# A layer kernel's stretch from the output projection to the third pair, written out in order, with the shift added in place on ScalarE and two weight blocks split ahead

## The chip, the cores and the metric

The kernel runs on one core of a Trainium2 chip. The metric is the device time of one execution in microseconds (us); the median of three runs stands for a kernel. A profile is taken of one execution; its durations are of that execution. A core has five engines that run their own instruction streams and wait for each other through semaphores: TensorE (PE, the matmuls), VectorE (DVE), ScalarE (ACT), GpSimd (POOL) and SyncE (SP, which here issues transfers). Matmuls accumulate in PSUM banks, all other tiles lie in SBUF.

## The reference, cut to what matters

One transformer layer on 512 latent tokens of width 2048. After the two attention branches come the output projection, a modulated norm and a gated MLP:

```
mod_x = (silu(c) @ w_ada + b_ada)                 # 6 x 2048 values
sh1, s1, g1, sh2, s2, g2 = split(mod_x, 6)
...
x = x + g1 * (merged_heads @ w_o)                 # output projection
h2 = rmsnorm(x, norm2_w) * (1 + s2) + sh2
g, u = split(h2 @ w_up, 2)                        # 2 x 5632 columns
g = conv3(g, conv_w) + conv_b                     # over tokens
x = x + g2 * ((silu(g) * u) @ w_down)
out = rmsnorm(x, final_w)
```

## The kernel before

**Numbers in two parts.** Activations are kept transposed: a tile is 128 features by 512 tokens. Every 32-bit matmul operand is split into a high part (a cast, on ScalarE) and a low part (the difference, on VectorE), and a product is three matmuls: high by high, weight high by activation low, weight low by activation high (`mm3`, L104 to L109). A weight block is 128 by 1024: `wblock` loads it (tile `wr`) and splits it (`wh`, `wl`; `split`, L80 and L81).

**Output projection (L1100 to L1125).** Four groups `g` of 512 output features, each over 8 weight blocks `kb`; a block is 24 matmuls of 512 columns. Between the blocks VectorE reduces rows of w_ada (`next_gemv`, L174), 28 of them in this loop, 7 in the last group. At a group's end VectorE adds the gated result to the residual (L1120, tiles `x1`), ScalarE squares it (L1083) and GpSimd sums the squares into `ss`; the last group's four squares are left for the norm.

**Norm (`token_norm`, L1086 to L1098).** A matmul with a matrix of ones sums `ss` and the last four squares over the features (L1090, L1094; 32-bit, two passes each), and `rstd` makes the inverse root: two ScalarE and four VectorE instructions (L162 to L167). The result is `nr`.

**First pair (`first_pair`, L1189 to L1205).** The MLP works on pairs `ft` of a 128-wide gate and a 128-wide value column block. The first two pairs are computed together, over 8 weight blocks taken as 0, 4, 1, 5, 2, 6, 3, 7; a block is 96 matmuls of 256 columns, since the left and right token halves (`h0`, `h1`) have operands of their own. Ahead of each half block `normed` (L1152) makes one feature tile `h` (L1156, VectorE), its high halves with the shift added (L1160, ScalarE) and its low halves (L1161, VectorE). `sums` (L1165) makes four combinations of the two token halves of tiles j and j+8 for later (`t1` to `t4`, each split), needed by the other pairs.

**Third pair and the rest.** Pair 2 is computed in the same way from four more blocks ("u" jobs). From pair 3 on a pair takes 7 products of half the size, Strassen-Winograd style ("p" jobs with k = 0 to 6), whose weight operands are blocks or sums of blocks (`weight_sum`, L1313). Products k = 0, 2 and 6 all add into one PSUM tile `y`; after k = 0 and k = 2 ScalarE copies `y` aside (`kept`, L1301, tile `m`), and the next product into `y` can only start after that copy. A gate goes through `gate_in` (L1214, ScalarE), `convolve` (L1219, L1221, VectorE), `silu` (L1226, ScalarE), `multiply` (L1230 VectorE, L1232 ScalarE) and `finish` (L1236, VectorE).

**What sets the order.** Up to the end of `first_pair` a scheduler places instructions on the engines, from the order of the code, pools and dependences. From L1293 on the order of PE, ACT, DVE and SP is that of the code: job i runs while `cast` (L1347) and `low` (L1353) split the weights of job i+2. Each engine takes its instructions strictly in order.

Of the kernel before, what the change touches and what calls it, by code (L numbers as in the profile page):

```python
# [17 lines left out]
P = 128  # L18
D = 2048
# [33 lines left out]
def layer_kernel(ctx: ExitStack, tc: tile.TileContext, small, rope, c_row, cc_row, x_t, ctx_t, ada, ada_k,  # L53
# [1009 lines left out]
    aq_ = tc.alloc_tile_pool(name="aq2", bufs=16, side="right", reuse_waits="tile")  # L1063

    def q2k(dt=F32):
        return aq_.tile([P, 512], dt, tag="q2k", name=nm("q2k"))

    wo = tc.alloc_tile_pool(name="wo", bufs=1, reuse_waits="tile")
# [4 lines left out]
    for h in range(16):  # L1073
        hl = a2k(F32R), q2k(F32R)
        split(hl[0], hl[1], oraw[h])
        osp.append(hl)

    def add_square(pool, ss, x, first):
        if first:
            sc.square(ss, x)  # L1080
        else:
            q = pool.tile([P, T], F32, tag="sq", name=nm("sq"), bufs=2)[:, :x.shape[1]]
            sc.square(q, x)  # L1083
            gp.tensor_tensor(out=ss, in0=ss, in1=q, op=ALU.add)

    def token_norm(pool, ss, last):  # L1086

        n = ss.shape[1]
        po = b_tile()[:, :n]
        pe.matmul(po, ones32, ss, start=True, stop=False)  # L1090
        for i, x in enumerate(last):
            q = pool.tile([P, T], F32, tag="h", name=nm("sq"), bufs=5)[:, :n]
            sc.square(q, x)
            pe.matmul(po, ones32, q, start=False, stop=i == len(last) - 1)  # L1094
        r = pool.tile([P, T], F32, tag="nr", name=nm("nr"), bufs=1)[:, :n]
        t1, t2 = (pool.tile([P, T], F32, tag="h", name=nm("n"), bufs=5)[:, :n] for _ in range(2))
        rstd(r, po, D, t1, t2)
        return r  # L1098

    x1, ss = [], wo.tile([P, T], F32, name="ss")  # L1100
    for g in range(4):
        if g % 2:
            outs = [b_tile() for _ in range(4)]
        else:
            s0, s1 = s_tile(), s_tile()
            outs = [s0[:, :512], s0[:, 512:], s1[:, :512], s1[:, 512:]]
        for kb in range(8):
            if kb > 2 and g == 0 or g in (1, 2) or kb < 7 and g == 3:
                next_gemv(wo, 1)
            wh, wl = wblock(w_o[g, kb])  # L1110
            order = [(j, i) for j in range(2) for i in range(4)]
            for j, i in sorted(order, key=lambda t: t[1]) if kb == 7 else order:
                kt, o = kb * 2 + j, j * 512 + i * P
                mm3(outs[i], (wh[:, o:o + P], wl[:, o:o + P]), osp[kt], kt == 0, kt == 15)
        for i in range(4):
            dt = g * 4 + i
            xr = wo.tile([P, T], F32, tag="xr", name=nm("xr"), bufs=6)
            nc.sync.dma_start(xr, x_t[dt])
            x = b2k()
            ve.scalar_tensor_tensor(out=x, in0=outs[i], scalar=modx[:, 32 + dt:33 + dt], in1=xr,  # L1120
                                    op0=ALU.mult, op1=ALU.add)
            x1.append(x)
            gp.dma_start(x1_d[dt], x)
            if g < 3:
                add_square(wo, ss, x, dt == 0)  # L1125
# [3 lines left out]
    db = sm.tile([P, 8], F32, name="db")  # L1129
    ve.tensor_tensor(db, modx[:, 56:64], modx[:, 48:56], op=ALU.add)  # L1130
    wo.release()
    ps_b.release()
    ps_s.release()
    nb[0] = 3
    ps_b = ctx.enter_context(tc.tile_pool(name="ps_m", bufs=4, space=PSUM, reuse_waits="tile"))

    ff = tc.alloc_tile_pool(name="ff", bufs=1, reuse_waits="tile")
    hp = tc.alloc_tile_pool(name="hp", bufs=1, side="right", reuse_waits="tile")
    h0, h1 = slice(0, HT), slice(HT, T)
    r = token_norm(hp, ss, x1[12:])
# [3 lines left out]


    hf, hx, t1, t2, t3, t4 = ([None] * KT for _ in range(6))  # L1150

    def normed(kt):  # L1152

        b = modx[:, 48 + kt:49 + kt]
        h = hf[kt] = hp.tile([P, T], F32, tag="h", name=nm("h"), bufs=5)
        ve.scalar_tensor_tensor(out=h, in0=x1[kt], scalar=a2[:, kt:kt + 1], in1=r, op0=ALU.mult, op1=ALU.mult)  # L1156
        hx[kt] = (a2k(F32R), q2k(F32R) if kt >= 8 else hp.tile([P, T], F32R, tag="h12", name=nm("h12"), bufs=8))
        for t, c in zip(hx[kt], (h0, h1)):
            hh, hl = half(t)
            sc.activation(hh, h[:, c], AF.Identity, bias=b)  # L1160
            ve.scalar_tensor_tensor(out=hl, in0=h[:, c], scalar=b, in1=hh.bitcast(F32), op0=ALU.add, op1=ALU.subtract)  # L1161

    spare = [tp.tile([P, T], F32R, tag="tp", name=nm("tp")) for _ in range(8)]

    def sums(j):  # L1165

        a, c, b = hf[j], hf[j + 8], modx[:, 56 + j:57 + j]
        d1, d2 = (hp.tile([P, HT], F32, tag="d", name=nm("d"), bufs=2) for _ in range(2))

        def put_away(t, src):  # L1170
            t[j] = q2k(F32R) if t is t1 else spare.pop(0) if spare else b2k(F32R)
            split(*half(t[j]), src)
# [507 lines left out]
```

## Time and profile before

| | |
|---|---|
| median of 3 runs | 2396.55 us (2394.12 to 2396.8) |
| the profiled execution: its own time | 2392.88 us |
| its span | 2391.1 us |
| granted TensorE clock, mean | 0.996 |
| last group's two last blocks, norm, first and third pair | about 990 to 1085 us of the span |

The page's first part gives the busy time of each engine over the span. PE is the engine with the largest share, and PEld (its weight loads) runs beside it. A timeline row gives start, duration, engine, line, operation, output and inputs, and in brackets the time for which the engine was idle just before and what it was released by. A window row gives length, then busy time with the number of instructions for PE, PEld, DVE, ACT and POOL, then the granted TensorE clock (1.00 is full), the share of the DMA engines that were busy, and GB/s.

### The profile page before, as it was taken

The page shows a single profiled execution, that of the slowest core. Times are in us where ns is not written, and L with a number is a line of the kernel's source. Part 1 is how long each engine was busy: PE and PEld are TensorE (multiplying, and loading weights), DVE is VectorE, ACT ScalarE, POOL GpSimd, SP SyncE. Part 2 cuts the span into 40 slices and gives each one's busy share as a digit, 9 for nine tenths or more (in the row PEclk, how much of TensorE's full clock was granted, in tenths as well). Part 3 has the DMA queues.
Part 4 walks back from the last instruction along what each step waited for, and adds up shares of the span by engine and source line. Part 5 has one row for each costly group of instructions (what it writes and reads, how often), then busy time and mean ns, then how long its engine had stood idle before and what let it go on. Part 6 is the DMA issues. An engine that isn't in the chain of part 4 may idle for free.

```text
span 2391.1 us, 32351 instructions
## 1 busy us (share of the span) xinstructions
PE 2331.0 (97%) x12444; PEld 1961.2 (82%) x12444; DVE 1778.5 (74%) x2303; ACT 1100.7 (46%) x1660; POOL 270.2 (11%) x322
## 2 busy tenths in 40 slices
PE   8999999999899999999999999999999999999997
PEld 5787888777677788798888888888888888888887
DVE  5996886798877877697585858575757676767767
ACT  4322322455555622364454545454545454445453
POOL 0011000121100011200101010101010101011113
PEclk9999999999999999999999999999999999999999
DMA  9767777853301289623646464546555545465572
GB/s 382 284 217 279 297 295 282 234 151 110 132 30 49 71 309 359 211 79 125 156 127 150 123 150 128 143 128 142 139 141 138 145 123 151 123 159 123 144 212 76
DMA packets 141515, 407.45 MB, mean 170 GB/s; under 512 B 14881, under 2 KB 31793, under 8 KB 130737
## 3 DMA queue, kind: packets, MB, share of 16 engines
q1 hardware_dynamic: 107584, 300.51, 37.9%
q0 software_dynamic: 32624, 103.83, 18.1%
q8 instruction: 97, 1.59, 0.3%
q10 hardware_dynamic: 1152, 1.05, 0.1%
q14 instruction: 58, 0.47, 0.1%
HBM read 335.86 MB, written 69.48 MB: 170 GB/s over the span
## 4 chain that ended last, share of the span: by engine, by line
PE 85%; DVE 8%; ACT 3%; issue 3%; DMA 1%; POOL 1%; DVEq 0%; SPq 0%; ACTq 0%; POOLq 0%
PE y L1377 13%; PE b L107 10%; PE b L108 10%; PE b L109 10%; PE z L1377 6%; PE y L1379 6%; PE z L1379 3%; PE s L883 3%; PE s L108 3%; PE s L107 3%; PE s L109 3%; PE x L1377 2%; PE x L1379 1%; PE pt L895 1%; PE f L107 1%
## 5 line engine op out<-in xcount | busy, mean ns | idle before, releaser
L1398 POOL DMA_DIRECT2D x_d<-xs x160 | 140.7, 1017 | 1160.4 <-ACT xs L1397 1140.8
L107 PE MATMUL b<-ah,wh 128*128 128x512 f32 (+1 forms) x672 | 259.1, 386 | 0.0
L108 PE MATMUL b<-al,wh 128*128 128x512 f32 (+1 forms) x672 | 259.0, 385 | 0.0
L109 PE MATMUL b<-ah,wl 128*128 128x512 f32 (+1 forms) x672 | 258.0, 384 | 0.0
L1353 DVE TENSOR_TENSOR wl<-rb,wh 128x1024 fp32r<-128x1024 f32 x124 | 151.2, 1220 | 128.7 <-ACT wh L1347 128.7
L1353 DVE TENSOR_TENSOR wl<-wr,wh 128x1024 fp32r<-128x1024 f32 x126 | 153.8, 1221 | 123.0 <-ACT wh L1347 123.0
L1347 ACT CAST wh<-wr 128x1024 fp32r<-128x1024 f32 x126 | 132.3, 1050 | 200.9 <-PE b L108 100.5
L1347 ACT CAST wh<-rb 128x1024 fp32r<-128x1024 f32 x124 | 130.2, 1051 | 191.7 <-PE b L108 116.1
L1353 DVE TENSOR_TENSOR wl<-ws,wh 128x1024 fp32r<-128x1024 f32 x123 | 150.1, 1221 | 89.2 <-ACT wh L1347 89.2
L174 DVE CUSTOM_DVE_ANT_0 ada<-ada,cb,smt 128x2048 f32<-128x2048 f32 x64 | 154.3, 2413 | 50.9 <-DMA ada<-in_ada 50.6
L1347 ACT CAST wh<-ws 128x1024 fp32r<-128x1024 f32 x123 | 128.3, 1043 | 135.7 <-PE b L108 45.4
L109 PEld LDWEIGHTS b<-ah,wl 128*128 128x128 f32 x672 | 126.3, 188 | 25.5
L107 PEld LDWEIGHTS b<-ah,wh 128*128 128x128 f32 x672 | 126.6, 188 | 22.9
L108 PEld LDWEIGHTS b<-al,wh 128*128 128x128 f32 x672 | 126.6, 188 | 22.0
L107 PE MATMUL b<-a2k,wh 128*128 128x512 f32 (+1 forms) x352 | 134.5, 385 | 7.3 <-ACT a2k L1160 5.0
L109 PE MATMUL b<-a2k,wl 128*128 128x512 f32 (+1 forms) x352 | 132.7, 377 | 0.7 <-DVE wl L402 0.6
L80 ACT CAST wh<-wr 128x1024 fp32r<-128x1024 f32 (+2 forms) x64 | 64.3, 1004 | 147.2 <-DMA wr<-in_w_o 45.7
L1377 PE MATMUL y<-b2k,wh 128*128 128x512 f32 x410 | 106.8, 390 | 0.0
L885 DVE TENSOR_REDUCE m<-s 128x1 f32<-128x768 f32 x96 | 90.2, 949 | 20.0 <-PE s L883 19.7
L81 DVE TENSOR_TENSOR wl<-wr,wh 128x1024 fp32r<-128x1024 f32 (+2 forms) x64 | 79.9, 1249 | 29.7 <-ACT wh L80 29.2
L1397 ACT ACTIVATE xs<-b,modx 128x512 f32<-128x512 f32 x160 | 101.0, 680 | 0.1
L210 ACT CAST wh<-wr 128x1024 fp32r<-128x1024 f32 x38 | 40.0, 1052 | 127.8 <-PE b L109 46.3
(536 smaller groups left out, 6080.5 us busy)
## 6 DMA issues: line engine op xcount, KB each, us to landing
rb<-in_w_up SPq DMA_DIRECT2D x123, 512.0 KB, 4.4
ada<-in_ada POOLq DMA_DIRECT2D x52, 1024.0 KB, 6.1
wr<-in_w_dn SPq DMA_DIRECT2D x84, 512.0 KB, 4.0
x_d<-xs POOLq DMA_DIRECT2D x160, 256.0 KB, 6.1
ada<-in_ada SPq DMA_DIRECT2D x28, 1024.0 KB, 6.9
wr<-in_w_up SPq DMA_DIRECT2D x53, 512.0 KB, 4.2
wr<-in_w_f SPq DMA_DIRECT2D x34, 512.0 KB, 5.9
adak<-in_ada_k SPq DMA_DIRECT2D x64, 256.0 KB, 5.4
```

The lines of the kernel that those rows point to most:

```text
L81: ve.tensor_tensor(dst_l, src, dst_h.bitcast(F32), op=ALU.subtract)
L107: pe.matmul(out, st[0], mv[0], start=start, stop=False, **kw)
L108: pe.matmul(out, st[0], mv[1], start=False, stop=False, **kw)
L109: pe.matmul(out, st[1], mv[0], start=False, stop=stop, **kw)
L174: ve.tensor_tensor_reduce(out=junk, in0=w, in1=vec, op0=ALU.mult, op1=ALU.add, scale=1.0, scalar=col("b_ada", j), accum_out=dst[:, j:j + 1])
L885: ve.tensor_reduce(out=m, in_=s[:, :TT], axis=AX.X, op=ALU.max, negate=True)
L1347: sc.copy(hi, raw)
L1353: ve.tensor_tensor(lo, raw, hi.bitcast(F32), op=ALU.subtract)
L1377: pe.matmul(o, w[j][0], hs[j], start=start and j == 0, stop=False, skip_group_check=True)
L1379: pe.matmul(o[:, h0], w[j][1], hs[j][:, h0], start=False, stop=j == 7, skip_group_check=True)
L1397: sc.mul(x, po, modx[:, 80 + dt:81 + dt])
L1398: gp.dma_start(x1_d[dt], x, accum_op=ALU.add)
```

## The change

- The order from the last group of the output projection to the third pair's last "u" block is now written out by hand (`every` engine), joined to the hand order that was there.
- In the last group, blocks 6 and 7 are run for the left token half first, then for the right. Residual, squares, ones matmuls, root and the first two normed pairs of tiles are done by halves too.
- `normed` now makes a pair of tiles: the norm, the left high half with bias, then the shift is added to the whole tile in place by ScalarE (`with_shift`, L1168), the right high half is a plain cast (L1184), and the low halves are plain differences (L1190). `sums` takes the shifted tiles, so its four combinations are plain additions and differences of 256 columns (L1204 to L1207); their splits are four casts and four differences in two separate pieces (`first`, `second`) that the order places with `some`.
- The third pair's first two weight blocks are loaded and split during the first pair. The loads of w_ada rows in the last group are issued ahead.
- The gates of the first three pairs, the weight sums and casts of pair 3 are placed by hand up to product k = 0 of pair 3 (`run(4)`); after it the loop is as before. The tile pools are cut differently to hold this.

The diff, cut to its core:

```diff
+
+    h0, h1 = slice(0, HT), slice(HT, T)
+    UP = [kb for j in range(4) for kb in (j, j + 4)]
...
+
+    def load8(i):
+        if i < len(src8):
+            raw8[i] = wraw(src8[i])
...
+        hl8[i] = [(pool or wp).tile([P, 1024], F32R, tag=g, name=nm(g), bufs=2 if pool else 3) for g in ("wh", "wl")]
+        sc.copy(hl8[i][0], raw8[i])
+
+    def low8(i):
+        ve.tensor_tensor(hl8[i][1], raw8.pop(i), hl8[i][0].bitcast(F32), op=ALU.subtract)
+        load8(i + 3)
+
...
-                mm3(outs[i], (wh[:, o:o + P], wl[:, o:o + P]), osp[kt], kt == 0, kt == 15)
+            out_block(outs, kb, wblock(w_o[g, kb]), skip=False)
+        if g == 2:
+            for i in range(2):
+                hl8[i] = wblock(src8[i])
         for i in range(4):
...
-            ve.scalar_tensor_tensor(out=hl, in0=h[:, c], scalar=b, in1=hh.bitcast(F32), op0=ALU.add, op1=ALU.subtract)
-
-    spare = [tp.tile([P, T], F32R, tag="tp", name=nm("tp")) for _ in range(8)]
+    hx, ht, t1, t2, t3, t4 = ([None] * KT for _ in range(6))
+
...
+    def norm_in(kt, c=slice(0, T)):
+        if ht[kt] is None:
+            ht[kt] = tp2k() if kt >= 8 else q2k(0)
+            hx[kt] = a2k(F32R), q2k(1, F32R) if kt >= 8 else hp.tile([P, T], F32R, tag="h12", name=nm("h12"), bufs=8)
+        ve.scalar_tensor_tensor(out=ht[kt][:, c], in0=x1[kt][:, c], scalar=a2[:, kt:kt + 1], in1=r[:, c],
+                                op0=ALU.mult, op1=ALU.mult)
+
+    def with_shift(kt):
+        sc.activation(ht[kt], ht[kt], AF.Identity, bias=shift(kt))
+
+    def normed_half(kts, c):
+        for kt in kts:
+            norm_in(kt, c)
+            sc.activation(half(hx[kt][c is h1])[0], ht[kt][:, c], AF.Identity, bias=shift(kt))
+        for kt in kts:
+            hh, hl = half(hx[kt][c is h1])
+            ve.scalar_tensor_tensor(out=hl, in0=ht[kt][:, c], scalar=shift(kt), in1=hh.bitcast(F32),
+                                    op0=ALU.add, op1=ALU.subtract)
+
+    def normed(kts, between=None):
+        for kt in kts:
+            norm_in(kt)
+            sc.activation(half(hx[kt][0])[0], ht[kt][:, h0], AF.Identity, bias=shift(kt))
+            with_shift(kt)
+            sc.copy(half(hx[kt][1])[0], ht[kt][:, h1])
+        if between:
+            between()
+        for kt in kts:
+            for t, c in zip(hx[kt], (h0, h1)):
+                hh, hl = half(t)
+                ve.tensor_tensor(hl, ht[kt][:, c], hh.bitcast(F32), op=ALU.subtract)
+
...
     def sums(j):
 
...
+        ds = []
+
+        def first():
+            a, c = ht[j], ht[j + 8]
+            d1, d2, d3, d4 = ds[:] = [d for _ in range(2) for d in half(scratch())]
+            ve.tensor_tensor(d1, c[:, h1], a[:, h1], op=ALU.add)
+            ve.tensor_tensor(d2, d1, a[:, h0], op=ALU.subtract)
+            ve.tensor_tensor(d3, a[:, h0], a[:, h1], op=ALU.subtract)
+            ve.tensor_tensor(d4, c[:, h0], d2, op=ALU.subtract)
+            t1[j], t3[j], t2[j], t4[j] = q2k(0, F32R), tp2k(F32R), b2k(F32R), b2k(F32R)
+            for t, d in zip((t1, t2, t3, t4), ds):
+                sc.copy(half(t[j])[0], d)
+
+        def second():
+            for t, d in zip((t1, t2, t3, t4), ds):
+                hh, hl = half(t[j])
+                ve.tensor_tensor(hl, d, hh.bitcast(F32), op=ALU.subtract)
+
+        return first, second
+
+    todo = [f for j in range(8) for f in sums(j)]
+
+    def some(count):
+        for _ in range(min(count, len(todo))):
+            todo.pop(0)()
+
...
+        for i in range(2):
+            load8(i + 2)
+            row_load()
+        load8(4)
+        outs = [b_tile() for _ in range(4)]
+        xrs = []
+        for i in range(6):
+            out_block(outs, i, hl8.pop(i))
+            cast8(i + 2)
+            low8(i + 2)
+            for _ in range(1 + (i == 2)):
+                row_sum()
+                row_load()
+            if i == 2:
+                xrs = [residual(12 + k) for k in range(4)]
+        assert next(gv, None) is None and not late_rows
+        wo.release()
+        hp = tc.alloc_tile_pool(name="hp", bufs=1, side="right", reuse_waits="tile")
+        r = ss
...
+        for kb in (6, 7):
+            out_block(outs, kb, hl8[kb], h0)
+        s0, s1 = s_tile(), s_tile()
+        fo = [s0[:, 512:], s1[:, :512], s1[:, 512:]]
+        sq = {}
+
+        def squares_of(c):
+            sq[c.start] = [t[:, k * HT:(k + 1) * HT] for t in (square_tile(), square_tile()) for k in range(2)]
+            for i in range(4):
+                evict(12 + i, outs[i], xrs[i], c)
+                sc.square(sq[c.start][i], x1[12 + i][:, c])
+
+        def ones_of(c):
+            qs = [ss[:, c]] + sq[c.start]
+            sq["po"] = s0[:, :HT] if c is h0 else b_tile()[:, :HT]
+            for q in qs:
+                pe.matmul(sq["po"], ones32, q, start=q is qs[0], stop=q is qs[-1], skip_group_check=True)
+
+        def root_of(c):
+            rstd(r[:, c], sq["po"], D, *half(scratch()))
+
...
-                kt = kb * 2 + j
-                normed(kt)
-                if n_ and n_ % 2 == 0:
-                    sums(n_ - 2 + j)
+                kt = UP[n_] * 2 + j
                 for i in range(4):
                     o = j * 512 + i * P
-                    classical(outs[i], kt, (wh[:, o:o + P], wl[:, o:o + P]), kt == 0, kt == KT - 1)
-        for j in (6, 7):
-            sums(j)
-        return [activate(ft, outs[2 * ft], outs[2 * ft + 1]) for ft in range(2)]
-
-    def activate(ft, g, u):
-
-        t = silu(convolve(ft, g))
-        return finish(t, multiply(t, u))
+                    classical(fo[i], kt, [t[:, o:o + P] for t in w], n_ == 0 and j == 0, n_ == 7 and j == 1, cs)
...
+        cast8(8)
+        low8(8)
+        cast8(9, ex)
+        low8(9)
+        squares_of(h0)
+        out_block(outs, 6, hl8[6], h1, js=(0,))
+        cast8(10, ex)
+        low8(10)
+        ones_of(h0)
+        out_block(outs, 6, hl8[6], h1, js=(1,))
+        root_of(h0)
+        out_block(outs, 7, hl8[7], h1)
+        normed_half(pair(0), h0)
+        fo.append(b_tile())
+        unit(0, (h0,))
+        squares_of(h1)
+        for i in range(4):
+            gp.dma_start(x1_d[12 + i], x1[12 + i])
+        normed_half(pair(1), h0)
+        ones_of(h1)
+        cast8(11)
+        root_of(h1)
+        unit(1, (h0,))
+        normed_half(pair(0), h1)
+        unit(0, (h1,))
+        normed_half(pair(1), h1)
...
+        unit(1, (h1,))
+        normed(pair(2), lambda: low8(11))
+        cast8(12)
+        for kt in (0, 1, 8, 9):
+            with_shift(kt)
+        for n_ in range(2, 8):
+            unit(n_, (h0, h1))
+            if n_ == 2:
+                ex.release()
+                wx.release()
+                ff = tc.alloc_tile_pool(name="ff", bufs=1, reuse_waits="tile")
+                ff.tile([P, T], F32R, tag="ah", name=nm("ah"), bufs=5)
+                ff.tile([P, T], F32R, tag="al", name=nm("al"), bufs=5)
+                rbp = tc.alloc_tile_pool(name="rbp", bufs=3, reuse_waits="tile")
+            if n_ < 7:
+                normed(pair(n_ + 1), lambda: low8(10 + n_))
+            else:
+                low8(17)
+            if n_ < 7:
+                cast8(11 + n_)
+            some((1, 1, 2, 1, 2, 3)[n_ - 2])
 
     def gate_in(ft, g):
-        t = ff.tile([P, T], F32, tag="t", name=nm("t"), bufs=1)
+        t = row_tile()
         sc.activation(t, g, AF.Identity, scale=col("cw", NFT + ft), bias=col("cb", ft))
         return t
 
...
-        cast(0)
-        low(0)
-        cast(1)
-        low(1)
-        rb.pump()
+        for i in range(2):
+            ready[i] = *hl8.pop(16 + i), None, None
+        for i in range(2):
+            run(i)
+            t = gate_in(i, fo[2 * i])
+            cast(i + 2)
+            convolve(i, fo[2 * i], t)
+            low(i + 2)
+            silu(t)
+            some(1)
+            acts[i] = multiply(t, fo[2 * i + 1])
+            some(i)
+            finish(t, acts[i])
+        run(2)
+        cast(4)
+        low(4)
+        some(3)
+        hp.release()
+        mm = tc.alloc_tile_pool(name="mm", bufs=1, side="right", reuse_waits="tile")
+        for g_, w_, n_ in (("ws", 1024, 2), ("m", T, 2), ("g", T, 1), ("u", T, 1)):
+            mm.tile([P, w_], F32, tag=g_, name=nm(g_), bufs=n_)
+        run(3)
+        cast(5)
+        low(5)
+        weight_sum(3, 1)
+        weight_sum(3, 2)
+        t = gate_in(2, live["s"][0])
+        cast(6)
+        convolve(2, live["s"][0], t)
+        low(6)
+        silu(t)
+        acts[2] = multiply(t, live["s"][1])
+        assert not todo
+        ps_b.release()
+        ps_s.release()
+        nb[0] = 3
+        ps_b = ctx.enter_context(tc.tile_pool(name="ps_m", bufs=4, space=PSUM, reuse_waits="tile"))
+        for g_ in (("y", 2), ("z", 2), ("x", 1)):
+            b_tile(*g_)
+        run(4)
+        finish(t, acts[2])
         for i, job in enumerate(jobs[:last]):
+            if i < 5:
+                continue
             run(i)
...
-            elif job == ("u", 3):
-                weight_sum(3, 1)
             cast(i + 2)
-            if i:
-                act_after(i - 1)
-                vec_after(i - 1)
+            act_after(i - 1)
+            vec_after(i - 1)
             low(i + 2)
```

PE, at the end of the output projection (`q2k` and `a2k` are the low and high parts of the attention output, `wh` and `wl` those of the weights, `ss` and `sq` the squares, `h` and the later `a2k` normed tiles). Before:

```order
L107 MATMUL b_8567<-a2k_7674,wh_8801 128x512
L108 MATMUL b_8567<-q2k_7675,wh_8801 128x512
L109 MATMUL b_8567<-a2k_7674,wl_8802 128x512
L1090 MATMUL b_8879<-ss,ones_85 128x512
L1094 MATMUL b_8879<-sq_8881,ones_85 128x512
L1094 MATMUL b_8879<-sq_8884,ones_85 128x512
L1094 MATMUL b_8879<-sq_8887,ones_85 128x512
L1094 MATMUL b_8879<-sq_8890,ones_85 128x512
L107 MATMUL b_8910<-a2k_8922,wh_8916 128x256
L107 MATMUL b_8911<-a2k_8922,wh_8916 128x256
```

The same place on PE in the change; the ones matmuls of the left half stand here inside block 6 of the right half (`t_7687` is the sum of squares):

```order
L108 MATMUL b_8619<-q2k_7672,wh_8787 128x256
L109 MATMUL b_8619<-a2k_7671,wl_8788 128x256
L1282 MATMUL s_8885<-t_7687,ones_85 128x256
L1282 MATMUL s_8885<-sq_8899,ones_85 128x256 x2
L1282 MATMUL s_8885<-sq_8900,ones_85 128x256 x2
L107 MATMUL b_8616<-a2k_7675,wh_8787 128x256
L108 MATMUL b_8616<-q2k_7676,wh_8787 128x256
L109 MATMUL b_8616<-a2k_7675,wl_8788 128x256
```

Behind these stand 36 more matmuls of the projection's right half, and then the first pair's left half. So between the ones matmuls and the first matmul that needs the root PE now has work of its own, where before the one followed the other directly.

ACT, where the third pair ends and pair 3 begins (`ah` is the high part of the third pair's result, `m` the copy of `y` after product k = 0, `wh` from `ws` and `rb` the casts of pair 3's weights). Before:

```order
L1347 CAST wh_9899<-ws_9897 128x1024
L1214 ACTIVATE t_9902<-y_9660,smt 128x512
L1226 ACTIVATE t_9902<-t_9902 128x512
L1347 CAST wh_9925<-ws_9870 128x1024
L1301 COPY m_9928<-y_9878 128x512
L1232 CAST ah_9931<-t_9902 128x512
L1347 CAST wh_9952<-rb_9654 128x1024
```

And in the change:

```order
L1348 ACTIVATE t_9988<-b_9686,smt 128x512
L1479 CAST wh_9990<-ws_9986 128x1024
L1360 ACTIVATE t_9988<-t_9988 128x512
L1366 CAST ah_9998<-t_9988 128x512
L1479 CAST wh_10046<-ws_9982 128x1024
L1433 COPY m_10049<-y_10009 128x512
L1479 CAST wh_10069<-rb_9680 128x1024
```

The cast to `ah`, which needs VectorE's multiplication (L1364), and one weight cast now stand ahead of the copy of `y`; before, the copy stood ahead of `ah`.

DVE at the same place, from the low half of pair 3's second weight block (`wl`, from `rb`) to the third pair's multiplication (`t`). Before:

```order
L1353 TENSOR_TENSOR wl_9875<-rb_9656,wh_9874 128x1024
L1320 TENSOR_TENSOR ws_9897<-rb_9658,ws_9870 128x1024
L1219 SCALAR_TENSOR_TENSOR t_9902<-y_9660,smt,t_9902 128x511
L1221 SCALAR_TENSOR_TENSOR t_9902<-y_9660,smt,t_9902 128x511
L1353 TENSOR_TENSOR wl_9900<-ws_9897,wh_9899 128x1024
L1323 TENSOR_TENSOR rb_9654<-rb_9658,rb_9654 128x1024
L1230 TENSOR_TENSOR t_9902<-t_9902,z_9661 128x512
```

In the change:

```order
L1485 TENSOR_TENSOR wl_9979<-rb_9682,wh_9978 128x1024
L1449 TENSOR_TENSOR ws_9982<-rb_9680,wr_9678 128x1024
L1452 TENSOR_TENSOR ws_9986<-rb_9684,ws_9982 128x1024
L1353 SCALAR_TENSOR_TENSOR t_9988<-b_9686,smt,t_9988 128x511
L1355 SCALAR_TENSOR_TENSOR t_9988<-b_9686,smt,t_9988 128x511
L1485 TENSOR_TENSOR wl_9991<-ws_9986,wh_9990 128x1024
L1364 TENSOR_TENSOR t_9988<-t_9988,b_9687 128x512
```

Inside this piece one weight sum (L1323, now L1455) has moved behind the multiplication. Just ahead of it stand, in the change, 12 rows of `sums` for tiles 6 and 7; before, the last row of `sums` stood six rows further up, inside the second pair's gate.

More of the change, by code (lines that the diff above doesn't have):

```diff
@@ L1073, in layer_kernel @@
     for h in range(16):
-        hl = a2k(F32R), q2k(F32R)
+        hl = a2k(F32R), q2k(h // 8, F32R)
         split(hl[0], hl[1], oraw[h])
         osp.append(hl)
[L1078 to L1098, printed above, removed]
@@ L1100, in layer_kernel, with square_tile, residual, evict @@
-    x1, ss = [], wo.tile([P, T], F32, name="ss")
-    for g in range(4):
+    def square_tile():
+        return wx.tile([P, T], F32, tag="sq", name=nm("sq"), bufs=2)
+    def residual(dt):
+        xr = wx.tile([P, T], F32, tag="xr", name=nm("xr"), bufs=6)
+        nc.sync.dma_start(xr, x_t[dt])
+        return xr
+    def evict(dt, out, xr, c=slice(0, T)):
+        ve.scalar_tensor_tensor(out=x1[dt][:, c], in0=out[:, c], scalar=modx[:, 32 + dt:33 + dt], in1=xr[:, c],
+                                op0=ALU.mult, op1=ALU.add)
```

150 lines of the change are left out of this document (71 added, 79 removed).

## The prediction

> **What bounds the kernel now.** I read the page's busy shares first, then the windows and the timeline of the stretch that the change writes anew, about 990 to 1090 us.
>
> ```profile
> PE 2331.0 (97%) x12444; PEld 1961.2 (82%) x12444; DVE 1778.5 (74%) x2303; ACT 1100.7 (46%) x1660; POOL 270.2 (11%) x322
> ```
>
> PE is the bound: only 60 us of the span are without a matmul. So a gain comes from an idle stretch of PE, a slow clock, or fewer matmuls. The timeline of PE (start, length, line, in brackets the idle time ahead and its releaser) shows such a stretch between the output projection and the first pair:
>
> ```profile
> 1001.56 0.40 PE L109 MATMUL b<-a2k,wl 128*128 128x512 f32 x1
> 1001.79 1.02 PE L1090 MATMUL b<-ss,ones 128*128 128x512 f32 x2
> 1003.39 3.70 PE L1094 MATMUL b<-sq,ones 128*128 128x512 f32 x8 [0.57 <-ACT sq L1093]
> 1012.12 0.79 PE L107 MATMUL b<-a2k,wh 128*128 128x256 f32 x2 [5.03 <-ACT a2k L1160]
> 1020.64 0.28 PE L107 MATMUL b<-a2k,wh 128*128 128x256 f32 x1
> ```
>
> PE is idle for 0.57 us before the squares and for 5.03 us before the first normed tile, 5.60 in all. The 48 matmuls of the first half block then take 1012.12 to 1020.64, 8.52 us. The windows (length, busy time of PE, PEld, DVE, ACT and POOL, granted clock, DMA share, GB/s) say why, and that VectorE is nearly full from here to 1072:
>
> ```profile
> 1013.00:1014.00 1.00, 1.00 (x6) 1.00 (x6) 1.00 (x3) 0.26 (x1) 0.00 (x0) 0.50 0.00 0
> 1018.00:1019.00 1.00, 1.00 (x10) 1.00 (x10) 1.00 (x4) 0.60 (x2) 0.00 (x0) 0.95 0.00 0
> 1020.00:1030.00 10.00, 10.00 (x85) 10.00 (x84) 8.86 (x20) 6.76 (x15) 0.00 (x0) 1.00 0.20 54
> 1030.00:1072.00 42.00, 41.61 (x347) 41.41 (x346) 41.81 (x87) 26.65 (x53) 0.00 (x0) 1.00 0.25 76
> 1072.00:1085.00 13.00, 13.00 (x110) 12.96 (x109) 7.49 (x9) 3.72 (x6) 0.00 (x0) 1.00 0.67 242
> ```
>
> After the idle stretch the clock is 0.50 until about 1018. At the pitch of 0.12 us that the full clock shows (1020.64 to 1020.76, below) 48 matmuls take 5.76, so the slow clock costs 2.76. From 1030 to 1072 PE and DVE are both full, 41.61 and 41.81 of 42.00. This is the row that decides: whoever removes PE's wait finds VectorE with no slack for 50 us, and then some slack (7.49 of 13.00) only after 1072.
>
> The other end of the section is product k = 2 of pair 3, from which on the order is that of before:
>
> ```profile
> 1020.76 0.28 PE L108 MATMUL b<-a2k,wh 128*128 128x256 f32 x1
> 1084.71 2.00 PE L1377 MATMUL y<-a2k,wh 128*128 128x512 f32 x8
> 1087.51 2.00 PE L1377 MATMUL x<-a2k,wh 128*128 128x512 f32 x8
> 1090.30 0.95 PE L1377 MATMUL y<-tp,wh 128*128 128x512 f32 x3
> ```
>
> I count time t from the start of block 6 of the last group. Blocks 6 and 7 are 48 matmuls at 0.2267 (1001.56 to 1001.79), so t = 0 is 1001.79 - 10.88 = 990.91, and k = 2 starts at **t = 99.4** before.
>
> **What PE could gain.** With work between the ones and the first normed tile, the 5.60 of idle and the 2.76 of slow clock go, 8.36. The two blocks in token halves are 96 matmuls of 0.12, 11.52 instead of 10.88, so -0.64. The ones matmuls took 1001.79 to 1007.09 less the 0.57, 4.73; in halves they are twice ten of 256 columns, by the end norm's row
>
> ```profile
> 2378.21 1.13 PE L1530 MATMUL b<-sq,ones 128*128 128x256 f32 x4 [0.49 <-ACT sq L1521]
> 2379.38 0.47 ACT L162 ACTIVATE ws<-b,epst 128x256 f32<-128x256 f32 x1 [0.83 <-PE b L1530]
> 2381.25 0.42 DVE L167 SCALAR_TENSOR_TENSOR ws<-ws 128x256 f32<-128x256 f32 x1
> ```
>
> about 0.22 each at its pitch, 4.4, so +0.3. The same rows give a root of half width as 2.3 us (2379.38 to 2381.67). Does the root hide? Left halves end at t = 5.8; 12 matmuls of block 6 (1.4), the ones (2.2), 36 more (4.3) carry PE to 13.7. Squares are done at 6.9, ones at 9.4, the root at 12.0, the first normed half at 13.1. It hides, by 0.6. The root of the right half is done at 21.4, and PE then waits 0.9 and 0.4 for the right halves of pair 0, later 0.4 and 1.4 for low parts of the normed tiles. These 3.1 stand against 0.4 of such waits in 1030 to 1072. Sum for PE: 8.36 - 0.64 + 0.3 - 2.7 = 5.3, so PE reaches k = 2 at t = 94.1 if nothing else holds it.
>
> **What VectorE and ScalarE can keep.** They hold k = 2, since it adds onto `y` and must wait until `m`, the copy of `y` after k = 0, is made. Durations, by line (minimum, median, maximum in ns) and from the page:
>
> ```profile
> L1156 DVE SCALAR_TENSOR_TENSOR h<-b2k,a,nr x16: 744/747/753, 1010.8 to 1057.5; 128x512 f32<-128x512 f32 x16
> L1161 DVE SCALAR_TENSOR_TENSOR a2k<-h,modx,a2k x16: 476/480/484, 1012.1 to 1059.2; 128x256 fp32r<-128x256 f32 x16
> L1160 ACT ACTIVATE a2k<-h,modx x16: 493/510/514, 1011.6 to 1058.2; 128x256 fp32r<-128x256 f32 x16
> L81 DVE TENSOR_TENSOR b2k<-d,b2k x16: 414/419/424, 1040.1 to 1072.4; 128x256 fp32r<-128x256 f32 x16
> L80 ACT CAST b2k<-d x16: 391/405/407, 1039.0 to 1071.9; 128x256 fp32r<-128x256 f32 x16
> L1226 ACT ACTIVATE t<-t x44: 627/632/640, 1065.7 to 2333.2; 128x512 f32<-128x512 f32 x44
> L1353 DVE TENSOR_TENSOR wl<-wr,wh 128x1024 fp32r<-128x1024 f32 x126 | 153.8, 1221 | 123.0 <-ACT wh L1347 123.0
> L1347 ACT CAST wh<-wr 128x1024 fp32r<-128x1024 f32 x126 | 132.3, 1050 | 200.9 <-PE b L108 100.5
> ```
>
> Back to back an engine issues somewhat faster than these lengths (0.08 less, as the 1.42 for two of L1156 in the row further below shows): 0.66 for a norm, 0.40 for a half with a scalar, 0.33 for a plain half, 1.13 for a low part of a block. What the trace lacks is the in-place addition of the shift on 128 by 512. Its nearest row is L1226, in place, 0.63; the half with bias (L1160) is 0.10 longer than the plain cast (L80), so 0.63 to 0.78, and I take 0.72. A hand-over between engines costs 0.04 (idle rows of the root: 2379.38 + 0.47 to 2379.89).
>
> Per pair of tiles VectorE saves: low parts without a scalar, 4 times 0.07; `sums` without scalars, some 0.07 on three of four instructions. But ScalarE gets 16 shifts, 11.5 us, and the order makes VectorE wait for them: left high, shift and right cast of both tiles of a pair run on ScalarE one after the other, with a hand-over each, and VectorE stands at the last differences. A pair is 0.79 until ScalarE starts, 0.54 + 0.76 + 0.32 for its first tile, 0.54 + 0.76 + 0.41 for the second and 0.36 for the last difference: **4.5**, of which VectorE works 3.8 (two norms, four differences, a weight's low part). Going down the written order:
>
> - right root 21.4; four norms and four lows of pairs 0 and 1: 25.1.
> - pair 2, 4.5; pair 3, 6.7, since four shifts of pairs 0 and 1 and a weight cast stand ahead of it on ScalarE: 36.3.
> - `sums` pieces 1.4 (four differences and the hand-over) or 1.3: with pairs 4 to 7 it is 1.4, 4.5, 1.3, 4.5, 2.7, 4.5, 1.4, 4.8, 2.7, to 64.1.
> - weights, gate and `sums` of the first of the two gates: 10.6, to 74.7; of the second: 8.0, to 82.7.
> - pair 3's first block: its cast waits for `sums` on ScalarE, 1.6 + 1.1, to 85.4; `sums` 6 and 7, 4.3, to 89.7; next low part 1.7, to 91.4; two weight sums 2.5, to 93.9; convolution 1.4, low 1.1, multiplication 0.7, to 97.1.
> - ScalarE: `ah` 0.6, cast 0.95, then `m` 0.6: done at **99.3**.
>
> In before the copy stood ahead of `ah`:
>
> ```profile
> 1010.77 1.42 DVE L1156 SCALAR_TENSOR_TENSOR h<-b2k,a,nr 128x512 f32<-128x512 f32 x2
> 1089.66 0.58 ACT L1301 COPY m<-y 128x512 f32<-128x512 f32 x1
> 1090.28 0.68 DVE L1230 TENSOR_TENSOR t<-t,z 128x512 f32<-128x512 f32 x1
> 1090.99 0.63 ACT L1232 CAST ah<-t 128x512 fp32r<-128x512 f32 x1 [0.75 <-DVE t L1230]
> ```
>
> There the multiplication came only at 1090.28, after the copy. Now copy, multiplication and `ah` are one chain, and k = 2 starts at t = 99.3: PE, ready at 94.1, waits 5.2 us. The gain of 5.3 is given back, -0.1 against 99.4. The bounds: with the shift at 0.63 I get 97.9, at 0.78 100.3; with hand-overs of 0.02 or 0.06, 98.1 or 100.6; with VectorE's pitches 0.015 off, 98.4 or 100.3. So -1.5 to +1.2. After k = 2 the order is as before and PE is the bound.
>
> **The clock.** PE's idle time before k = 2 is as long as the one before the first pair, 5.03, and that one cost 2.76 of half clock behind it. Shorter idle times go both ways in this trace:
>
> ```profile
> 47.76 0.38 PE L107 MATMUL b<-c2k,wh 128*128 128x256 f32 x1 [1.58 <-ACT c2k L236]
> 49.00:50.00 1.00, 1.00 (x7) 1.00 (x6) 1.00 (x3) 0.74 (x2) 0.00 (x0) 0.50 0.97 391
> 657.48 0.73 PE L883 MATMUL s<-krh,qs 128*128 128x512 f32 x2 [2.91 <-DMA krh<-kr_d]
> 658.00:659.00 1.00, 1.00 (x8) 0.96 (x8) 0.00 (x0) 0.00 (x0) 0.00 (x0) 1.00 0.06 16
> ```
>
> After 1.58 us the clock was 0.50, after 2.91 it stayed 1.00. For the new wait the nearest row is the 5.03, so I take +2.8, bounds 0 and 2.8. Nothing hides it, since PE is the bound from there on.
>
> The Trainium skill ("TensorE: Matmul & The Clock Gate", section "Why this matters for your kernels") says that a gap of more than about 3 us between bursts of matmuls puts TensorE back to half clock. The 5.03 and the 2.91 agree with it; the 1.58 at 47.76 does not. By it the new wait halves the clock and the waits of up to 1.4 do not: the sum as above, +2.7; with a clock that a single gap left alone it would be -0.1.
>
> **Transfers.** The last group needs the same blocks and its 7 rows, only their issue is earlier; two weight blocks come some 30 us sooner, in a stretch where the DMA share is 0.25. I cost them at nothing; a late row would hold block 6 by about 1 us, which the wait at k = 2 would swallow.
>
> **Sum.** -0.1 + 2.8 = +2.7: 2392.88 becomes about 2395.6 for an execution like the profiled one. The median of before lies 3.67 above it, so I add the difference to the median: 2396.55 + 2.7 = 2399.2. Own range 2395.0 to 2400.6 from the bounds.
>
> **Rivals.**
> - **VectorE and ScalarE keep up (0.18).** If ScalarE's shifts overlap better than I string them, or `m` comes before t = 94, k = 2 does not wait. Then the 5.3 stay, 2391.2; without the small waits too, 8.0, 2388.5. Against it: DVE's 41.81 of 42.00. For it: VectorE's own work falls, by some 4 us (32 and 24 instructions by 0.07).
> - **The clock stays full after the new wait (0.12).** 2396.5, no change. The 2.91 row speaks for it, the 5.03 row against.
> - **ScalarE's chain is longer still (0.12).** The shift at 0.78, hand-overs of 0.06 and pitches 0.015 up together put `m` at 99.3 + 1.0 + 1.3 + 1.0 = 102.6, +3.2, with the clock +6.0: 2402.6. It decides from t = 101.4 on, where with the clock the loss is 4.8.
> - The forecast holds 0.58.
>
> Faster and slower are counted from 0.2%, 4.8 us, about what a measurement of this kernel can tell from no change. Faster is the first rival, 0.18. Slower is the last rival and a sixth part of its chance again from the forecast's own upper end with a noisy median, in all 0.16. The rest, 0.66, is the same. The range takes most of the first rival and of the last: 2389.0 to 2403.0.
>
> **What would show it.** The root hidden: no idle time of PE over 1 us ahead of the first pair, and a clock of 1.00 there. The new wait: one row of PE at k = 2 (L1509, `y`) with some 5 us idle, released by ACT's copy `m` (L1433), and windows at 0.50 behind it. VectorE idle ahead of the last differences (L1190) of every pair, by 0.6 us or more. The prediction is wrong if that row is missing or PE waits there under 2 us; or if a new wait shows earlier, for a weight block or a row of w_ada.

## The result and the profile after

The changed kernel is slower: 2407.51 us median (2406.39 to 2414.28) against 2396.55, ratio 1.0052 with a 95% interval of 1.0032 to 1.0072. The profiled execution has a span of 2404.5 us against 2391.1, 13.4 us more. The range on record, 2389.0 to 2403.0, does not hold it.

The stretch that the prediction worked out came as forecast, and it is not where the time went. The timeline of PE in the changed kernel, with the waits that are left there (no idle time ahead of the first normed tile):

```profile
1000.76 0.28 PE L107 MATMUL b<-a2k,wh 128*128 128x256 f32 x1
1022.79 0.39 PE L107 MATMUL s<-h,wh 128*128 128x256 f32 x1 [0.66 <-ACT h L1173]
1040.93 0.39 PE L108 MATMUL s<-a2k,wh 128*128 128x256 f32 x1 [0.34 <-DVE a2k L1190]
1054.03 0.38 PE L108 MATMUL s<-a2k,wh 128*128 128x256 f32 x1 [1.21 <-DVE a2k L1190]
1099.88 3.78 PE L1509 MATMUL y<-b2k,wh 128*128 128x512 f32 x8 [5.85 <-ACT m L1433]
1104.95 2.03 PE L1509 MATMUL z<-q2k,wh 128*128 128x512 f32 x8
```

The first row is the first of block 6, so t = 0 is 1000.76; product k = 2 starts at 1099.88, t = 99.1, after a wait of 5.85 us for the copy `m`. The chain of waits of that stretch, in order of time (start, length, engine and line), shows the chain that the prediction strung together:

```profile
1092.09 1.23 DVE ws L1449
...
1093.34 1.23 DVE ws L1452
1094.57 0.67 DVE t L1353
...
1095.93 1.22 DVE wl L1485
1097.14 0.61 DVE t L1364
...
1097.78 0.62 ACT ah L1366
1098.39 0.95 ACT wh L1479
1099.34 0.49 ACT m L1433
```

Behind the wait the clock is at half, by the windows (columns as before):

```profile
1095.00:1099.00 4.00, 0.00 (x0) 0.00 (x0) 3.28 (x5) 2.56 (x4) 0.00 (x0) 0.86 0.27 105
1102.00:1103.00 1.00, 1.00 (x3) 0.74 (x3) 1.00 (x2) 0.00 (x0) 0.00 (x0) 0.50 0.00 0
1104.00:1105.00 1.00, 1.00 (x8) 1.00 (x8) 0.00 (x0) 0.78 (x1) 0.00 (x0) 0.66 0.89 332
```

The loss lies ahead of it: block 6 starts 9.85 us later than before (990.91). The first matmul of the attention (L883) is late already, long before any line that the diff touches. First the row of the kernel before, then that of the change:

```profile
431.78 0.47 PE L883 MATMUL s<-ks,qs 128*128 128x512 f32 x1
```

```profile
436.27 0.39 PE L883 MATMUL s<-ks,qs 128*128 128x512 f32 x1
```

And in the projection PE is busy throughout in both, at full clock, but does fewer matmuls in the same time; the window 900 to 930 of before, then of the change:

```profile
900.00:930.00 30.00, 30.00 (x134) 24.84 (x133) 24.62 (x23) 7.62 (x10) 9.85 (x8) 1.00 0.95 358
```

```profile
900.00:930.00 30.00, 30.00 (x130) 24.13 (x129) 24.03 (x20) 8.63 (x10) 9.86 (x8) 1.00 0.93 355
```

The timeline gives the step. A block is 24 matmuls; before, block 7 runs from 996.35 to 1001.79, 0.2267 each; in the change block 5 runs from 995.16 to 1000.76, 0.2333 each:

```profile
996.35 0.39 PE L107 MATMUL b<-a2k,wh 128*128 128x512 f32 x1
...
1001.79 1.02 PE L1090 MATMUL b<-ss,ones 128*128 128x512 f32 x2
```

```profile
995.16 0.39 PE L107 MATMUL b<-a2k,wh 128*128 128x512 f32 x1
```

| place | before | after | later by |
|---|---|---|---|
| first matmul of the attention | 431.78 | 436.27 | 4.5 |
| block 6 of the last group | 990.91 | 1000.76 | 9.85 |
| product k = 2 of pair 3 | 1090.30 | 1099.88 | 9.6 |
| product k = 3 of pair 3 | 1093.19 | 1104.95 | 11.8 |
| span | 2391.1 | 2404.5 | 13.4 |

So some 10 us are lost ahead of the rewritten stretch, about 0 in it, 2.2 to the clock behind the new wait, 1.6 in the loop and the end. The 4902 matmuls ahead of block 6 are the same in both traces and can be compared one by one. Of the 9.85, the 3095 of 512 columns at full clock took 9.4 us longer, half clock added 1.3, and waits were 0.8 shorter. The half clock is another matter: near 115 us PE waits 2.86 us before and 2.84 us in the change, and behind it the clock stayed full in the one and was halved in the other (windows of before, then of the change); it was halved there in e1 below too, which has the weights back in their places:

```profile
115.00:121.00 6.00, 6.00 (x34) 5.25 (x35) 5.96 (x8) 0.00 (x0) 0.53 (x1) 1.00 0.64 229
```

```profile
115.00:121.00 6.00, 5.69 (x17) 4.82 (x18) 5.94 (x8) 0.26 (x1) 0.19 (x1) 0.50 0.64 231
```

The 1.6 behind k = 2 is a change of pace too, a smaller one: there 4191 matmuls of 512 columns took 4.8 us longer (1.1 ns each), 2656 of 256 columns 2.9 us less, and waits 0.3 less.

What reaches so far back? One removed line of the diff: `db = sm.tile([P, 8], F32, name="db")`. The pool `sm` lies under nearly all other pools on the left side of SBUF, so everything above it moved down by 32 bytes (8 columns of 4 bytes). Read from the built programs, the three tiles `wh` start at multiples of 512 bytes before and 32 bytes below such multiples in the change, and the tiles of the attention output, on the right side, did not move; no trace prints these addresses, and the experiments test what follows from them.

### The profile page after: what moved, and what is told of

Read it like the earlier page. It is cut to its first block, busy times and chain, and to the rows that moved or that the text cites. A ratio compares the mean times of both kernels' runs of the same rounds, so it can differ in the third digit from the quotient of the medians.

```text
span 2404.5 us, 32481 instructions
## 1 busy us (share of the span) xinstructions
PE 2342.8 (97%) x12502; PEld 1960.2 (82%) x12502; DVE 1777.2 (74%) x2314; ACT 1112.3 (46%) x1682; POOL 268.8 (11%) x322
## 4 chain that ended last, share of the span: by engine, by line
PE 80%; DVE 10%; ACT 4%; issue 3%; DMA 2%; POOL 1%; SPq 0%; DVEq 0%; ACTq 0%; POOLq 0%
PE y L1509 11%; PE b L107 10%; PE b L108 10%; PE b L109 10%; PE z L1509 6%; PE y L1511 6%; PE s L108 3%; PE s L109 3%; PE s L107 3%; PE s L883 3%; PE z L1511 3%; PE x L1509 2%; PE pt L895 1%; DVE wl L1485 1%; PE x L1511 1%
## 5 line engine op out<-in xcount | busy, mean ns | idle before, releaser
L174 DVE CUSTOM_DVE_ANT_0 ada<-ada,cb,smt 128x2048 f32<-128x2048 f32 x57 | 135.8, 2385 | 55.9 <-DMA ada<-in_ada 55.8
L80 ACT CAST wh<-wr 128x1024 fp32r<-128x1024 f32 (+2 forms) x50 | 49.5, 990 | 113.9 <-DMA wr<-in_w_o 52.9
L1509 PE MATMUL y<-b2k,wh 128*128 128x512 f32 x328 | 85.5, 403 | 9.1 <-ACT m L1433 9.1
L107 PE MATMUL s<-a2k,wh 128*128 128x512 f32 (+1 forms) x240 | 90.2, 376 | 0.0
```

The source lines that it names most:

```text
L107: pe.matmul(out, st[0], mv[0], start=start, stop=False, **kw)
L174: ve.tensor_tensor_reduce(out=junk, in0=w, in1=vec, op0=ALU.mult, op1=ALU.add, scale=1.0, scalar=col("b_ada", j), accum_out=dst[:, j:j + 1])
L1509: pe.matmul(o, w[j][0], hs[j], start=start and j == 0, stop=False, skip_group_check=True)
```

## The experiments

Two theories. **Layout**: the 32 bytes change where weights lie against the moving operand, and that slows the 512-column matmuls. **Order**: the new order and its transfers slow PE. Each kernel was timed against the kernel before, whose median was 2396.08 us beside e1 to e3, 2396.44 beside e4, e5 and e8, and 2394.35 beside e7.

**e1, the 32 bytes put back into the change.**

```diff
+    sm.tile([P, 8], F32, name="db")
```

> The change with 32 bytes put back where the tile db was (an unused tile of 8 columns), so that tiles start at multiples of 64 bytes again. Layout theory: the 512-column matmuls of the projection come every 0.2267 us again instead of 0.2333, block 6 of the last group starts near 991 us instead of 1000.8, and the time falls by about 11 us from 2407.5 to 2396 to 2399. Order theory (the written order itself is slow): pitch and time as in the change, 2407.

Measured 2399.04 (2394.21 to 2403.41), ratio 1.0011 (1.0000 to 1.0023). Block 5 is back at 5.44 for 24 matmuls, 0.2267, and block 6 starts at 991.1; the wait for `m` is still there. PE rows of e1:

```profile
985.68 0.39 PE L107 MATMUL b<-a2k,wh 128*128 128x512 f32 x1
991.12 0.28 PE L107 MATMUL b<-a2k,wh 128*128 128x256 f32 x1
...
998.90 0.39 PE L107 MATMUL b<-a2k,wh 128*128 128x256 f32 x1 [1.87 <-DVE b2k L1096]
...
1092.69 3.78 PE L1511 MATMUL y<-b2k,wh 128*128 128x512 f32 x8 [5.55 <-ACT m L1435]
```

The layout theory holds: 8.5 us of the change's loss, of about 11 expected, hang on 32 unused bytes. The row at 998.90 is new. VectorE waited for the last row of w_ada until 993.75, 2.6 us behind the start of block 6, where in the change it was 0.15 us behind; so it read the left halves late in this execution, and k = 2 came at t = 101.6.

**e2 and e3, the kernel before with nothing but a shift.** An unused tile at the bottom of the pool `sm` is made 32 (e2) or 64 (e3) bytes shorter:

```diff
-    sm.tile([P, 64], F32, name="edge")
+    sm.tile([P, 56], F32, name="edge")
```

> The kernel before with an unused tile 32 bytes shorter, so that all later tiles of that side move by 32 bytes, and nothing else. Layout theory: pitch 0.2333 in the projection, block 6 of the last group 9 to 10 us later, time 2405 to 2408. Order theory: 2396.5, unchanged.

> The kernel before with the same tile 64 bytes shorter, so all tiles move but keep their start modulo 64. If only the start modulo 64 matters: unchanged, 2396.5, pitch 0.2267. If any move away from the former addresses costs: about 2406.

e2: 2405.87 (2403.22 to 2412.22), ratio 1.0039 (1.0025 to 1.0053). e3: 2401.61 (2398.08 to 2409.89), ratio 1.0023 (1.0011 to 1.0036). The last projection block, of e2 and then of e3:

```profile
1011.69 0.40 PE L107 MATMUL b<-a2k,wh 128*128 128x512 f32 x1
...
1017.28 1.02 PE L1090 MATMUL b<-ss,ones 128*128 128x512 f32 x2
```

```profile
1002.24 0.39 PE L107 MATMUL b<-a2k,wh 128*128 128x512 f32 x1
...
1007.74 1.02 PE L1090 MATMUL b<-ss,ones 128*128 128x512 f32 x2
```

5.59 and 5.50 for 24, 0.233 and 0.229. Block 6 of e2 came at 1006.09, 15.2 us later than before and not the 9 to 10 expected. Matched with before, its 512-column matmuls at full clock account for 8.8 of it; half clock, as in the window below, for 5.6; longer waits for 1.3.

```profile
617.00:623.00 6.00, 6.00 (x17) 4.83 (x18) 3.15 (x7) 2.53 (x5) 0.00 (x0) 0.50 0.70 282
```

The shift alone, without any change of order, makes the kernel before about as slow as the changed one. But the start modulo 64, which e3 keeps, is not what counts: e3 lies between.

**m1 and m2, the pace by itself.** Matmuls alternate two weight tiles and two moving tiles, in the order of `mm3`.

> Matmuls alone (the layer is left out): per case 96 of 512 and 96 of 256 columns, with the weight tile and the moving tile starting 0, 16, 32 or 64 bytes past a multiple of 64. Layout theory by the weights: 0.2267 for weights at 0 and 64, 0.2333 at 32, whatever the moving tile. By the moving tile: the other way. Order theory: all cases 0.2267. For 256 columns the change's trace lets expect 0.117 with weights at 32 against 0.120 at 0.

m1 missed: no case showed 0.2267. For 512 columns the first case ran mostly at half clock, and the seven others lie, by the starts of the records, at 0.231 to 0.233; for 256 columns all eight lie at about 0.118. By the sizes of the tiles, the second weight tile and the two moving tiles started 128, 256 and 384 bytes, modulo 512, past the first weight tile, so that every case mixed several distances. m2 puts all tiles on multiples of 512 bytes first.

> Matmuls alone (the layer is left out), tiles now at multiples of 512 bytes, 192 of 512 and 96 of 256 columns per case; weights and moving tile start (0,0), (480,0), (448,0), (256,0), (128,0), (0,480), (480,480), (0,256) bytes past such a multiple. If the weights' start against the moving tile's modulo 512 sets the pace: (0,0) 0.2267, (480,0) 0.2333, (448,0) 0.2289 for 512 columns as in the whole kernels, and 0.120, 0.117, 0.118 for 256; equal shifts of both (480,480) 0.2267 if only the difference counts, 0.2333 if the weights' own start counts. If the pace of the whole kernels comes from other traffic: 0.2267 in all cases.

The windows of m2, 30 us inside the 512-column part of the cases (0,0), (480,0), (448,0), (256,0), (128,0), (0,480), (480,480), (0,256), the count behind the first busy time being the matmuls that touch the window:

```profile
80.00:110.00 30.00, 30.00 (x134) 24.84 (x133) 0.00 (x0) 0.00 (x0) 0.00 (x0) 1.00 0.00 1
140.00:170.00 30.00, 30.00 (x130) 24.08 (x129) 0.00 (x0) 0.00 (x0) 0.00 (x0) 1.00 0.00 1
200.00:230.00 30.00, 30.00 (x132) 24.61 (x132) 0.00 (x0) 0.00 (x0) 0.00 (x0) 1.00 0.00 1
260.00:290.00 30.00, 30.00 (x134) 24.83 (x133) 0.00 (x0) 0.00 (x0) 0.00 (x0) 1.00 0.00 1
320.00:350.00 30.00, 30.00 (x131) 24.32 (x130) 0.00 (x0) 0.00 (x0) 0.00 (x0) 1.00 0.00 1
380.00:410.00 30.00, 30.00 (x131) 24.13 (x130) 0.00 (x0) 0.00 (x0) 0.00 (x0) 1.00 0.00 1
439.00:469.00 30.00, 30.00 (x134) 24.85 (x133) 0.00 (x0) 0.00 (x0) 0.00 (x0) 1.00 0.00 1
499.00:529.00 30.00, 30.00 (x134) 24.85 (x133) 0.00 (x0) 0.00 (x0) 0.00 (x0) 1.00 0.00 1
```

By the starts of the records the steps are, in ns: 226.7, 233.3, 228.9, 226.7, 232.4, 233.3, 226.7, 226.7. No other engine and no transfer is at work. So the whole kernels' three paces are reproduced, and where both weight tiles start alike modulo 512, and both moving tiles too, it is the distance between the starts of weights and moving tile that sets them: moving the one by 480 costs as much as moving the other, moving both costs nothing, and 0 and 256 apart are equal. For 256 columns it is the other way: 120.0 at 0 or 256 apart, 117.8 to 118.7 elsewhere. What inside the chip makes it so, these runs don't show. Nor do they give a rule for tiles that start differently: in m1's case with both starts moved alike, half of the matmuls had weights and moving tile 256 bytes apart and the others 128, which by m2 would make 0.2295 on average, and 0.232 was measured.

**e4, the copy `m` ahead of the cast to `ah`, on top of e1.**

```diff
-        acts[2] = multiply(t, live["s"][1])
+        ve.tensor_tensor(t, t, live["s"][1], op=ALU.mult)
...
         run(4)
+        act_after(4)
+        acts[2] = [ff.tile([P, T], F32R, tag=g_, name=nm(g_), bufs=5) for g_ in ("ah", "al")]
+        sc.copy(acts[2][0], t)
         finish(t, acts[2])
```

> As e1_pad_back (2399.0), but ScalarE copies y aside ahead of the cast to ah, as in the kernel before. If the place of the copy behind the multiplication and ah is what holds product k = 2: it starts about 2.7 us earlier, PE's wait there falls from 5.55 to about 2.9, and the time to about 2396 (2394 if the clock then stays full). If the wait is set by something ahead of the copy that this edit does not move (a weight cast, PE itself): unchanged, 2399.

2393.81 (2389.41 to 2397.89), ratio 0.9988 (0.9978 to 0.9998); the wait is 2.94 as forecast (timeline of e4, first), and the clock 0.66 in the 5 us from 1090 on (windows, second):

```profile
1090.88 1.65 PE L1511 MATMUL y<-b2k,wh 128*128 128x512 f32 x3 [2.94 <-ACT m L1435]
```

```profile
1090.00:1095.00 5.00, 4.12 (x14) 3.40 (x15) 4.32 (x6) 3.43 (x6) 0.00 (x0) 0.66 0.00 1
```

So the place of the copy was part of what gave the gain back. The time fell by 5.2 against e1, more than the 2.6 of the wait. In the profiled executions product k = 3 starts 106.7 us behind block 6 in e1 and 101.1 here, 5.6 less: 2.6 is the wait for `m`, 0.8 the shorter half clock, and by 2.2 PE came earlier to k = 2, mostly since the wait at 998.90 (1.87) is absent. How many executions of e1 had that wait is not on record, so how much of the 5.2 the place of the copy alone is worth isn't shown.

**e5, the in-place shift undone, on top of e1**: bias in both high halves, the shift as a scalar in VectorE's low halves and `sums`, as before.

```diff
-            with_shift(kt)
-            sc.copy(half(hx[kt][1])[0], ht[kt][:, h1])
+            sc.activation(half(hx[kt][1])[0], ht[kt][:, h1], AF.Identity, bias=shift(kt))
...
-                ve.tensor_tensor(hl, ht[kt][:, c], hh.bitcast(F32), op=ALU.subtract)
+                ve.scalar_tensor_tensor(out=hl, in0=ht[kt][:, c], scalar=shift(kt), in1=hh.bitcast(F32),
+                                        op0=ALU.add, op1=ALU.subtract)
```

> As e1_pad_back, but without the in-place shift on ScalarE: bias in both high halves, shift as a scalar in VectorE's low halves and sums, as in the kernel before. If ScalarE's 16 shifts set the length of the chain: PE's waits at the low parts of the normed tiles (0.3 to 1.2 us) go, and k = 2 starts 4 to 5 us earlier, 2394. If VectorE's own work is the bound and the shifts only fill its gaps: k = 2 starts about 2 us earlier, with the wait there still over 5 us, since PE also comes earlier; time about 2397.

2396.52 (2391.61 to 2401.76), ratio 1.0000 (0.9988 to 1.0011). The small waits at the low halves are gone, the big one is not:

```profile
1089.45 2.93 PE L1510 MATMUL y<-b2k,wh 128*128 128x512 f32 x6 [5.29 <-ACT m L1434]
```

The wait and the time fit the second reading. The start of k = 2 is less clear: counted from block 6 (at 992.17) it is t = 97.3, 4.3 us earlier than in e1, whose late row is in that, but only 1.8 earlier than in the change. In the change VectorE stood idle for 5.0 us at the shifts (L1168); in e5 some 1.6 us of other idle time and 1.6 us of longer instructions stand in their place. So the shifts lengthened the chain by some 2 us, and the rest of it does not depend on them.

**e8, both, and the last of the `sums` later.** The differences of tile 7 now stand behind the third pair's convolution, their casts and low halves behind the copy `m` (`act_after(4)`).

```diff
         low(4)
-        some(3)
+        some(1)
...
         weight_sum(3, 2)
         t = gate_in(2, live["s"][0])
         cast(6)
         convolve(2, live["s"][0], t)
+        silu(t)
+        some(1)
         low(6)
-        silu(t)
-        acts[2] = multiply(t, live["s"][1])
+        ve.tensor_tensor(t, t, live["s"][1], op=ALU.mult)
...
         run(4)
+        act_after(4)
+        some(1)
```

> As e5_shift_undone, and the third pair's gate, pair 3's weight sums and the copy of y stand ahead of the last of the sums (tile 7), whose casts and low parts follow behind the copy. If the chain to the copy is what gives the gain back: no wait at k = 2, a full clock behind it, three new waits of 0.5 to 1 us in the next products, and 2390 to 2392, below the kernel before. If the waits only move: one wait of 3 us or more in pair 3 with a half clock behind it, 2396 or more.

2392.12 (2387.55 to 2399.0), ratio 0.9986 (0.9974 to 0.9998), the fastest of all and a little faster than the kernel before. No wait at k = 2, three behind it that are mostly smaller than the 0.5 to 1 us expected, and a clock of 1.00 from 1085 to 1105:

```profile
1090.79 1.21 PE L1518 MATMUL z<-q2k,wl 128*128 128x256 f32 x8 [0.31 <-DVE wl L1492]
1092.22 2.12 PE L1516 MATMUL y<-tp,wh 128*128 128x512 f32 x8 [0.22 <-ACT m L1440]
1095.92 2.14 PE L1516 MATMUL z<-b2k,wh 128*128 128x512 f32 x8 [0.64 <-ACT m L1440]
```

**e7, the order of e8 with the in-place shift of the change.**

> As e8_reordered (2392.1), but with the change's in-place shift on ScalarE. If the shifts cost only where they delay the copy, which the new order now takes out of the way: small waits of 0.3 to 1.2 us come back at the low parts of the normed tiles, and 2393 to 2394. If the shifts are the main cost of the change: 2397 or more.

2392.31 (2389.86 to 2398.84), ratio 0.9991 (0.9979 to 1.0002). The waits at the low parts are back, 1.2 us the longest. Against the kernel before beside it the gain is 2.0 us, where e8 had 4.3, but the intervals overlap: once the copy no longer waits, the shift on ScalarE costs nothing that these runs can tell.

## Why the prediction was wrong, step by step

- **PE's gain**: right. The 5.60 us of idle time and the slow clock went, the root hid. The small waits were forecast as 0.9 + 0.4, 0.4 and 1.4; they were 0.66, 0.34 and 1.21.
- **The chain to `m`**: right. The in-place shift, estimated at 0.72 between 0.63 and 0.78, took 0.72:

```profile
L1168 ACT ACTIVATE q2k<-q2k,modx x8: 707/723/725, 1026.8 to 1054.0; 128x512 f32<-128x512 f32 x8
```

  k = 2 was forecast at t = 99.3 and came at 99.1; the wait was 5.85 instead of 5.2, since PE arrived 0.8 earlier, its 256-column matmuls coming every 0.117 instead of 0.120. VectorE did stand at the last differences (L1190) of every pair, but in four of the six for 0.46 to 0.48 us, less than the 0.6 named as a sign.
- **The reason given for the chain**: half right. I laid its length to VectorE standing at ScalarE's shifts; e5 shows that without them k = 2 comes only 1.8 us earlier than in the change, counted from block 6, and still waits 5.29.
- **The clock**: right in kind. k = 2 took 5.07 (1099.88 to 1104.95) instead of 2.89 (1090.30 to 1093.19), 2.2 lost where I took 2.8. The Trainium skill ("TensorE: Matmul & The Clock Gate", section "Why this matters for your kernels") advises against idle gaps of more than about 3 us between bursts of matmuls. The 5.85 agrees with that; near 3 us the traces go both ways: e4's 2.94 and the change's 2.84 near 115 us lowered the clock, the 2.91 near 657 us and the 2.86 near 115 us in the kernel before did not.
- **The sum**: this step failed. "2392.88 becomes about 2395.6" adds the stretch's -0.1 and the clock's 2.8 to a kernel whose other parts keep their time; t was counted from block 6, and block 6 was left at 990.91 without a word. It moved by 9.85, and the loop after k = 2, called "as before", by 1.6, since the 512-column matmuls ahead of block 6 took 9.4 us longer (0.2333 instead of 0.2267 each in the projection) and those of the loop 4.8, of which its 256-column matmuls gave 2.9 back. The line that did it, the removed `db`, stood in the diff as one row of bookkeeping. With the 32 bytes back (e1) the median is 2399.04, against a forecast of 2399.2; that they agree so closely is luck, with runs from 2394.21 to 2403.41 and a late row of w_ada in the profiled one.
- **Rivals**: none named this. The slower one (ScalarE's chain longer still, 2402.6) would have shown `m` after t = 101.4; it was at 99.1. Its chance of 0.12 and a sixth of that are 0.14, not the 0.16 given for "slower".
- **Transfers at nothing**: held in the change, where PE was slow enough. In e1 one late row cost PE 1.87 in the profiled execution, and the wait at k = 2 did not swallow it, since VectorE's chain started late as well.

What stays open: why the distance of two starts sets the pace, what tiles of mixed starts do, and the 1.3 us between e1's gain of 8.5 and the 9.8 that the shift cost the kernel before, which the spread of the runs covers.

## What to carry to other kernels

A tile removed from a pool that others stand on moves them all: compare the operands' start addresses of the two built programs before believing that untouched code keeps its time. Where matmuls of 512 columns bound a kernel, keep all weight and moving tiles at the same start modulo 256, and check the step between matmuls in one untouched stretch of the trace first. And removing a wait of the bound engine only pays if the chain behind the next one it meets, here a copy queued behind work that did not need to precede it, is shortened as well.

## What was not expected of the hardware

At a full clock and with PE never idle, one and the same matmul of 512 columns came every 226.7, 228.9, 232.4 or 233.3 ns, by nothing but the distance between the starts of weights and moving tile (0, 64, 128 and 32 bytes apart modulo 256). Over the 720 matmuls of the projection's full-width blocks 6.7 ns each are 4.8 us. For 256 columns the placement that is best for 512 is the slower one, 120.0 against 117.8 ns.
